# Later modulation weights with buffers and sums of their own, and stores and dependent loads issued from ScalarE's queue

## The chip, the cores and the metric

One core of a Trainium2 chip runs one program. The metric is the device time of a run in microseconds (us); of several runs the median is taken. The engines are TensorE (PE, matmuls; its weight loads are PEld), VectorE (DVE), ScalarE (ACT), GpSimd (POOL) and SyncE (SP), which here only issues DMAs. Each engine works its own list of instructions in order; semaphores hold an instruction until what it needs is there. TensorE's clock stands at one of two levels, 1.2 and 2.4 GHz; the profile gives the granted clock of a stretch as a share of the higher one.

## What is computed

One transformer block on 1024 tokens of 1024 channels, in float32. `dwconv` is a causal convolution along the tokens with one filter per channel, `wkv7_scan` a recurrence over the tokens with one 64x64 state per head (8 heads):

```python
mod = silu(c) @ ada_w + ada_b                 # 6 vectors of 1024
sh_m, sc_m, gt_m, sh_f, sc_f, gt_f = split(mod, 6)
h = rms_norm(x, mix_pre_g) * (1 + sc_m) + sh_m
p = h @ w_in                                  # u, u_gate | r, k, v, wd, ad, gd
u = silu(layer_norm(dwconv(u * sigmoid(u_gate), 31 taps)) * g + b)
r, k, v, ... = shift_mix(p)                   # p + (previous token's p - p) * mu
decay, a, kk = f(w0 + tanh(wd) @ w2), sigmoid(a0 + ad @ a2), unit(k * k_k)
y = layer_norm(wkv7_scan(r, decay, k, v, kk, a)) ; y = (y + bonus) * (sigmoid(gd) @ g2)
x = x + gt_m * rms_norm(concat(u, y) @ w_out, mix_post_g)
h = rms_norm(x, ffn_pre_g) * (1 + sc_f) + sh_f
z = dwconv(h @ w_up, 3 taps)                  # 2 x 2816 channels
x = x + gt_f * rms_norm((silu(z_gate) * z_val) @ w_down, ffn_post_g)
```

## The kernel before

**Layout.** Channels lie on the 128 partitions, tokens along the free axis, in two halves of 512 tokens. A tile of a projection is 128 output channels by 512 tokens in one PSUM bank. Float32 is reached by splitting each operand in a high and a low part: per 128 input channels three matmuls (lines 158 to 160), 24 for a tile of w_in. `weight` (line 134) fetches half a tile's weights, 128x512 or 256 KB: a DMA on SP (line 138), a cast to the high part on ScalarE (140), the low part on GpSimd (142). It draws on a pool of three buffers for each of the tags w, wh and wl, so at most three halves are under way.

**Modulation.** `mod` has twelve column blocks of 512, two (z = 0, 1) for each of the six vectors. Each is the sum of eight products: load a 128x512 slab of ada_w (line 226), multiply it by a column of silu(c) and add it to a running sum (lines 235 and 237, VectorE), then sum over the partitions with four matmuls against ones (`adr...`, line 243) and add the bias (244). The blocks of sh_m and sc_m come first, in `start`. The other eight blocks, 64 loads and products, are a generator, `spare`: `project` takes `rate` steps of it with each half of a tile (line 153). Groups 0 to 2 (gt_m, sh_f, sc_f; 48 loads) begin with the gated tiles of half 0, at three steps a half, later one; group 3 (gt_f, 16 loads) begins with the up-projection of half 0. Their slabs use the pool of three of the projection weights (tag w), their sum lies in SBUF (`cacc_b`), and their column sums take one of the two PSUM banks of tag m.

**Stages and order.** Half 0: `start`, six tiles begun early (`p_first`), `lora` (la), `in_group` for two groups of heads (k, v, r; `p_k`, `p_v`, `p_r`), gates (gd, ge), then four pairs of gated convolution tiles (`glu`: p_ug, p_u), whose result u goes to DRAM (line 320) and comes back with its edge as `cu` (line 333). Then the same for half 1, with the 31 taps of half 0's convolution as filler (`conv`: three channel tiles on VectorE with the sum in PSUM, line 344, one on ScalarE and GpSimd).

The recurrence runs in four units of 256 tokens, at the scheduler's highest priority. `unit` does, for two groups of heads, `prep` (decay w and a, line 492; scaled r, k, kk; score blocks s, line 550, stored to DRAM, 556), `inverse` (a triangular inverse done on blocks that are loaded in another layout, ab, line 575, and stored, sd, line 617), `finish` of the unit before (norm, bonus and gate: loads at 723 and 727, stores to `mixed` at 730) and `merge` (loads dd of the inverse, line 625, matmuls pt, 630, and hn, 637). `chain` then takes four steps (ch, lines 679 and 684; y, 692 to 702), each needing the state of the one before. Then out_proj of half 0 (stores md, 779), `channel_in` (residual, norm; stores x1d, 795), `up` of half 0: 44 tiles with 3-tap convolutions on VectorE and GpSimd, whose 22 products are stored (act, line 842), interleaved with the convolution of half 1; out_proj and channel_in of half 1, `down` of half 0, `up` and `down` of half 1.

**What sets the order.** A scheduler places each engine's instructions in one fixed list; `first()` and `high_priority` raise a stretch. A PSUM bank or an SBUF buffer is handed to its users in the order in which the program is written. PSUM has eight banks: tag m two, w two, and s, c, y and v one each. All DMAs shown here are issued by SP before the change.

Of the kernel before, what the change touches and what calls it, by code (L numbers as in the profile page):

```python
# [67 lines left out]
def build(nc, tc, I, O):  # L68
# [151 lines left out]
    def ada_cols(j, src, name, pool, tag, bufs, apool, atag, b="m", share=()):  # L220
# [23 lines left out]
        V.tensor_tensor(mod[:, j:j + 4], ps[:, 0:4], col("ada_b", j, 4), ALU.add)  # L244

    h = [None] * NK
    started = {}
# [65 lines left out]
    def glu(h, half, ct):  # L313
        pg = in_tile(h, 2 * ct + 1, f"ug{half}_{ct}")
        sg = tmp(f"sg{half}_{ct}")
        S.activation(sg, pg, AF.Tanh, scale=0.5, bias=ZERO)
        pu = in_tile(h, 2 * ct, f"u{half}_{ct}")
        u = tmp(f"u{half}_{ct}")
        V.scalar_tensor_tensor(u, sg, 1.0, pu, ALU.add, ALU.mult)
        nc.sync.dma_start(ud[half][ct], u)  # L320
        next(filler[0], None)
# [47 lines left out]
    def conv_norm(accs, half, b):  # L369
# [14 lines left out]
        for ct in range(4):  # L384
            V.tensor_tensor(accs[ct], accs[ct], rb, ALU.mult)
            t = slot(cv, "ctmp", f"th{half}_{ct}", bufs=2)
            S.activation(t, accs[ct], AF.Tanh, scale=col("ln_g", ct), bias=col("ln_b", ct))
            S.activation(accs[ct], accs[ct], AF.Identity, scale=col("ln_g", ct), bias=col("ln_b", ct))
            V.scalar_tensor_tensor(accs[ct], t, 1.0, accs[ct], ALU.add, ALU.mult)
            nc.sync.dma_start(mixed[half][ct], accs[ct])  # L390

# [35 lines left out]
    def gate_out(parts, half):  # L427
# [7 lines left out]
        for p in range(4):  # L435
            gb = bank(f"gt{half}{p}", "m")
            o = slice(p * P, (p + 1) * P)
            TE.matmul(gb, wh[:, o], gh, start=True, stop=False)
            TE.matmul(gb, wh[:, o], gl, start=False, stop=False)
            TE.matmul(gb, wl[:, o], gh, start=False, stop=False)  # L440
            TE.matmul(gb, w3[:, o], e3, start=False, stop=True)
            t = tmp(f"gt{half}_{p}")
            S.copy(t, gb)
            nc.sync.dma_start(gated[half][p], t)

# [31 lines left out]
    def prep(q, g, kvr, la, pcs, sa):  # L477
# [63 lines left out]
        s.bv = dr.tile([P, HT], F32, name=f"bvd{n}", tag="bvd", bufs=4)  # L541
        nc.sync.dma_start(s.bv, bv)

# [11 lines left out]
        for r, hh in HS:  # L555
            nc.sync.dma_start(sa[2 * g + hh].rearrange("c s t -> s c t"), at[r])

# [11 lines left out]
    def inverse(q, sa, sdg):  # L569
# [4 lines left out]
        for b in range(4):  # L574
            nc.sync.dma_start(ab3[b * 32:b * 32 + 32], sa5[b, b])
        dp = wk.tile([P, 528], F32, name=f"dm{q}", tag="dm", bufs=1)
# [37 lines left out]
        for x in range(2):  # L614
            sx = sdg[x].rearrange("q c (b r) (e t) -> b e (q c) r t", b=4, e=4)
            for b in range(4):
                nc.sync.dma_start(sx[b, b], dm[x][b * 32:b * 32 + 32])

    def merge(gs, sdg):

        for s in gs:
            s.dd = dd = wk.tile([P, 2, 8, 64], F32, name=f"dd{s.n}", tag="bk", bufs=2)
            for x in range(2):
                for r, hh in HS:
                    nc.sync.dma_start(dd[r, x], sdg[x, 2 * s.g + hh].rearrange("c r t -> r c t"))  # L625
        for s in gs:
# [81 lines left out]
    def finish(q, gs, ys):  # L708
# [11 lines left out]
        for s, y in zip(gs, ys):  # L720
            n = s.n
            bv = slot(rw, "t", f"bvl{n}", bufs=2)
            nc.sync.dma_start(bv, s.bv)
            gt = slot(rw, "t", f"gtl{n}", bufs=2)
            for i in range(2):
                p, o = 2 * s.g + i, slice(i * QT, (i + 1) * QT)
                nc.sync.dma_start(gt[:, o], gated[half][p][:, t0:t0 + QT])
                V.scalar_tensor_tensor(y[:, o], y[:, o], col("lnx_g", p), bv[:, o], ALU.mult, ALU.add)
                V.scalar_tensor_tensor(y[:, o], y[:, o], col("lnx_b", p), gt[:, o], ALU.add, ALU.mult)
                nc.sync.dma_start(mixed[half][4 + p][:, t0:t0 + QT], y[:, o])  # L730

# [39 lines left out]
    def out_proj(half, ins):  # L771

        acc = None
        for m in range(8):
# [3 lines left out]
            S.copy(t, ps)  # L778
            nc.sync.dma_start(md[half][m], t)
            acc = square_sum(acc, t, m, f"o{half}")  # L780
        return acc

    def channel_in(half, acc, b):
# [4 lines left out]
        for k in range(8):  # L788
# [5 lines left out]
            (V, G)[half == 0 and k % 2].tensor_tensor(t, t, xs[k], ALU.add)  # L794
            nc.sync.dma_start(x1d[half][k], t)
            acc = square_sum(acc, t, k, f"f{half}")
# [33 lines left out]
    def up(h, half, at=lambda j: None):  # L830

        acts = []
        for j in range(NU):
# [7 lines left out]
            if half == 0:  # L841
                nc.sync.dma_start(ad[j], g_)
            else:
# [45 lines left out]
    vt = v_tiles(0)  # L889
    kvrs = [in_group(h, 0, g, vt[g]) for g in range(2)]  # L890
    zero = tmp("zero", HT)
# [7 lines left out]
    with first():  # L899
        u0 = unit(0, kvrs, la)  # L900
        ys, zv = chain(0, *u0, None)
    ada = lambda gs: (x for g in gs for z in range(2)
                      for x in ada_cols(16 + 8 * g + 4 * z, I["ada2"][g, z], f"b{g}{z}", wp, "w", 3, cv, "cacc2"))
    spare, rate = ada(range(3)), 3
    for ct in range(4):
# [8 lines left out]
    for x in xs:  # L914
        V.tensor_tensor(x, x, rb, ALU.mult)
    h = [modulate(x, gm[:, k:k + 1], mod[:, k:k + 1], f"1_{k}") for k, x in enumerate(xs)]
    accs = [None] * 4
    rate = 1
# [18 lines left out]
    with first():  # L937
# [3 lines left out]
        finish(3, u3[0], ys)  # L941
    for _ in spare:
        pass
    gains()
# [4 lines left out]
    accs = [None] * 4  # L949
    spare = ada((3,))  # L950
    filler[0] = conv(1, accs, 3)
    up(h, 0, lambda j: j == 18 and conv_norm(accs, 1, "s"))
    V.tensor_tensor(gpf, mod[:, 40:48], col("ffn_post_g", 0, 8), ALU.mult)
# [70 lines left out]
```

## Time and profile before

| | |
|---|---|
| median of three runs | 1517.69 us (1516.13 to 1522.84) |
| profiled execution | 1514.99 us |
| its span | 1513.2 us |
| TensorE busy | 1377.6 us (91%), mean granted clock 0.949 |
| VectorE busy | 958.3 us (63%) |
| ScalarE busy | 645.9 us (43%) |
| GpSimd busy | 796.4 us (53%) |

The span is the time from the first to the last instruction in the profile. Busy shares are means over stages that have different limits; DMA issues and waits do not count as busy. The matmul of 512 columns is listed with some 0.39 us but the next starts 0.23 us after it, since they are pipelined.

### The profile page before, as it was taken

How to read it: one execution, taken by the hardware profiler on the slowest of the kernel's cores; microseconds unless marked ns; L12 is line 12 of the kernel's file. 1: busy time of each engine (PE TensorE's matmuls, PEld its weight loads, DVE VectorE, ACT ScalarE, POOL GpSimd, SP SyncE). 2: the span in 40 equal slices, each digit the busy share in tenths (PEclk: the TensorE clock that was granted, in tenths of full speed). 3: DMA queues.
4: the chain of work that ended last, by engine and by line, in shares of the span. 5: the costliest groups of instructions: out<-in, count | busy, mean ns of one | idle time of the engine just before them, and what ended most of it. 6: DMA issues, size and time to landing. Idle time of an engine off the chain costs nothing.

```text
span 1513.2 us, 22723 instructions
## 1 busy us (share of the span) xinstructions
PE 1377.6 (91%) x8148; PEld 1111.8 (73%) x8148; DVE 958.3 (63%) x1449; ACT 645.9 (43%) x1126; POOL 796.4 (53%) x710
## 2 busy tenths in 40 slices
PE   3999868789889999769999999999998999999995
PEld 2777657677667777657788887788886888888884
DVE  8657857969989576587889965557117555552102
ACT  5344322355534454344455555654233444443221
POOL 2555413676755346435577764446545555554443
PEclk9998998899999999869999999999999999999997
DMA  9153645533224544834444335884335333333332
GB/s 358 58 167 101 176 140 160 175 81 105 63 60 118 162 138 107 219 116 128 138 132 133 118 120 179 303 274 134 101 97 185 98 97 97 97 95 93 94 95 73
DMA packets 161761, 203.78 MB, mean 135 GB/s; under 512 B 63536, under 2 KB 70320, under 8 KB 161648
## 3 DMA queue, kind: packets, MB, share of 16 engines
q1 hardware_dynamic: 161648, 202.33, 43.4%
q8 instruction: 64, 1.05, 0.3%
q14 instruction: 49, 0.40, 0.1%
HBM read 168.19 MB, written 34.08 MB: 134 GB/s over the span
## 4 chain that ended last, share of the span: by engine, by line
PE 66%; DVE 17%; DMA 10%; issue 3%; SPq 2%; POOL 2%; ACT 1%; DVEq 0%; POOLq 0%; ACTq 0%
PE up L158 10%; PE up L159 9%; PE up L160 9%; PE d L159 5%; PE d L160 5%; PE d L158 5%; DMA w_adb<-ada 3%; DVE cv L344 2%; PE o L159 2%; PE o L158 2%; PE o L160 2%; DMA aw_ada<-ada 2%; DVE cacc_b L237 1%; DVE rkp L528 1%; SPq L625 1%
## 5 line engine op out<-in xcount | busy, mean ns | idle before, releaser
L142 POOL TENSOR_TENSOR wl_up<-w_up,wh_up 128x512 fp32r<-128x512 f32 x176 | 240.3, 1370 | 157.5 <-ACT wh_up L140 150.7
L158 PE MATMUL up<-hh_f,wh_up 128*128 128x512 f32 x704 | 278.6, 396 | 10.2 <-DVE q_za L815 7.0
L159 PE MATMUL up<-hl_f,wh_up 128*128 128x512 f32 x704 | 277.0, 394 | 0.0
L160 PE MATMUL up<-hh_f,wl_up 128*128 128x512 f32 x704 | 276.6, 393 | 0.0
L140 ACT CAST wh_up<-w_up 128x512 fp32r<-128x512 f32 x176 | 108.7, 619 | 187.0 <-PE up L159 127.6
L142 POOL TENSOR_TENSOR wl_dn<-w_dn,wh_dn 128x512 fp32r<-128x512 f32 x96 | 116.9, 1220 | 118.0 <-ACT wh_dn L140 112.0
L158 PEld LDWEIGHTS up<-hh_f,wh_up 128*128 128x128 f32 x704 | 133.9, 190 | 40.6 <-issue 9.8
L160 PEld LDWEIGHTS up<-hh_f,wl_up 128*128 128x128 f32 x704 | 133.6, 190 | 28.2 <-issue 0.2
L159 PEld LDWEIGHTS up<-hl_f,wh_up 128*128 128x128 f32 x704 | 133.7, 190 | 27.6
L159 PE MATMUL d<-al,wh_dn 128*128 128x512 f32 x352 | 139.4, 396 | 0.0
L160 PE MATMUL d<-ah,wl_dn 128*128 128x512 f32 x352 | 139.4, 396 | 0.0
L158 PE MATMUL d<-ah,wh_dn 128*128 128x512 f32 x352 | 139.2, 395 | 0.0
L344 DVE SCALAR_TENSOR_TENSOR cv<-cu,pv,cv 128x512 f32<-128x512 f32 x174 | 130.4, 749 | 2.4
L140 ACT CAST wh_dn<-w_dn 128x512 fp32r<-128x512 f32 x96 | 56.1, 584 | 151.3 <-PE d L159 123.7
L860 DVE TENSOR_SCALAR mo_f<-d,mod 128x512 f32<-128x512 f32 x16 | 12.0, 749 | 170.4 <-ACT q_sqd L859 159.1
L810 DVE SCALAR_TENSOR_TENSOR q_za<-up,pv,q_za 128x510 f32<-128x510 f32 x88 | 65.6, 746 | 78.4 <-ACT q_za L808 78.4
L352 POOL TENSOR_TENSOR cacc<-cacc,ctmp 128x512 f32<-128x512 f32 x60 | 79.1, 1318 | 42.3 <-ACT ctmp L351 38.7
L159 PEld LDWEIGHTS d<-al,wh_dn 128*128 128x128 f32 x352 | 66.2, 188 | 16.0
L160 PEld LDWEIGHTS d<-ah,wl_dn 128*128 128x128 f32 x352 | 66.2, 188 | 15.8
L158 PEld LDWEIGHTS d<-ah,wh_dn 128*128 128x128 f32 x352 | 66.2, 188 | 15.8
L838 DVE SCALAR_TENSOR_TENSOR q_za<-q_th,q_za 128x512 f32<-128x512 f32 x44 | 57.7, 1312 | 30.3 <-ACT q_th L837 30.3
L815 DVE SCALAR_TENSOR_TENSOR q_za<-up,pv,q_za 128x511 f32<-128x511 f32 x88 | 65.9, 748 | 14.0 <-ACT carry_z L814 8.3
(383 smaller groups left out, 3024.5 us busy)
## 6 DMA issues: line engine op xcount, KB each, us to landing
w_up<-w_up SPq DMA_DIRECT2D x176, 256.0 KB, 2.8
w_dn<-w_down SPq DMA_DIRECT2D x80, 256.0 KB, 2.7
w_adb<-ada SPq DMA_DIRECT2D x64, 256.0 KB, 3.0
aw_ada<-ada SPq DMA_DIRECT2D x32, 256.0 KB, 5.4
w_o<-w_out SPq DMA_DIRECT2D x32, 256.0 KB, 3.5
act<-q_za SPq DMA_DIRECT2D x22, 256.0 KB, 2.0
ax<-act SPq DMA_DIRECT2D x22, 256.0 KB, 4.2
w_ug<-w_in SPq DMA_DIRECT2D x16, 256.0 KB, 3.1
```

Of the source, the lines that this page charges most:

```text
L140: S.copy(hi, w)
L142: e.tensor_tensor(lo, w, hi.bitcast(F32), ALU.subtract)
L158: TE.matmul(ps, wh[:, o], xh, start=k == 0, stop=False)
L159: TE.matmul(ps, wh[:, o], xl, start=False, stop=False)
L160: TE.matmul(ps, wl[:, o], xh, start=False, stop=k == K - 1)
L237: V.scalar_tensor_tensor(acc, w, sc[:, k:k + 1], acc, ALU.mult, ALU.add)
L344: yield V.scalar_tensor_tensor(o, u[:, k:k + HT], cw(ct, k), acc, ALU.mult, ALU.add)
L352: G.tensor_tensor(acc, acc, t, ALU.add)
L528: V.tensor_tensor(pic(rkp[x][:, :, 1 + hh, :])[r], part(kkn, x)[r], half(eprev, x)[r], ALU.mult)
L810: V.scalar_tensor_tensor(a[:, 2:], ps[:, 0:HT - 2], fw(0), a[:, 2:], ALU.mult, ALU.add)
L815: V.scalar_tensor_tensor(a[:, 1:], ps[:, 0:HT - 1], fw(1), a[:, 1:], ALU.mult, ALU.add)
L838: V.scalar_tensor_tensor(g_, t, 1.0, g_, ALU.add, ALU.mult)
```

## The change

Two things are done at once. First, the later modulation weights get a generator of their own, `ada_rest`. Groups 0 to 2 load into five buffers of the convolution's pool that are free until `conv` starts, four loads ahead; group 3 into three buffers of tag k, two ahead. The running sum lies in PSUM (bank v, for group 3 bank c), the last product writes it to SBUF for the column sums, which now use the default bank tag, s, of one buffer. The generator is begun before the second `in_group` of half 0 with one step for each half of a tile, two in `glu`, and is emptied before half 0's convolution; group 3 begins at tile pair 8 of the up-projection. Second, at fifteen places `nc.sync.dma_start` becomes `S.dma_start`: the stores of u (line 320), of the mixed convolution (390), gated (444), bvd (542), sa (556), sd (617), mx (730), md (779), x1d (795) and act (842), and the loads ab (575), dd (625), bvl (723) and gtl (727), all of which wait for something computed. In SP's list 156 rows go and in ScalarE's 156 come. Lines of the changed kernel behind 245 have numbers higher by 31, from 888 on by some 40.

```diff
+    def ada_rest(groups, slab, ahead, last, b):
+
+
+        todo = [(g, z, k) for g in groups for z in range(2) for k in range(NK)]
+        tiles = {}
+
+        def fetch(i):
+            if i < len(todo):
+                g, z, k = todo[i]
+                tiles[i] = slab(i, f"adb{g}{z}_{k}")
+                nc.sync.dma_start(tiles[i], I["ada2"][g, z, k])
+
+        for i in range(ahead):
+            fetch(i)
+        for i, (g, z, k) in enumerate(todo):
+            fetch(i + ahead)
+            w, name = tiles.pop(i), f"b{g}{z}"
+            if k == 0:
+                acc = bank(f"ad{name}", b)
+                V.tensor_scalar(acc, w, sc[:, 0:1], None, ALU.mult)
+            else:
+                o = last(name) if k == NK - 1 else acc
+                V.scalar_tensor_tensor(o, w, sc[:, k:k + 1], acc, ALU.mult, ALU.add)
+            if k == NK - 1:
+                j = 16 + 8 * g + 4 * z
+                ps = bank(f"adr{name}")
+                for m in range(4):
+                    TE.matmul(ps[:, m:m + 1], o[:, m * P:(m + 1) * P], ones, start=True, stop=True)
+                V.tensor_tensor(mod[:, j:j + 4], ps[:, 0:4], col("ada_b", j, 4), ALU.add)
+            yield
...
             for b in range(4):
-                nc.sync.dma_start(sx[b, b], dm[x][b * 32:b * 32 + 32])
+                S.dma_start(sx[b, b], dm[x][b * 32:b * 32 + 32])
...
                 for r, hh in HS:
-                    nc.sync.dma_start(dd[r, x], sdg[x, 2 * s.g + hh].rearrange("c r t -> r c t"))
+                    S.dma_start(dd[r, x], sdg[x, 2 * s.g + hh].rearrange("c r t -> r c t"))
...
             if half == 0:
-                nc.sync.dma_start(ad[j], g_)
+                S.dma_start(ad[j], g_)
...
-    kvrs = [in_group(h, 0, g, vt[g]) for g in range(2)]
+    kvrs = [in_group(h, 0, 0, vt[0])]
+
+    ctags = ("ctmp", "cu", "ctmp", "cu3", "cacc0")
+    spare = ada_rest(range(3), lambda i, n: slot(cv, ctags[i % 5], n, 30 + HT if ctags[i % 5][:2] == "cu" else HT,
+                                                 2 if ctags[i % 5] == "ctmp" else 1)[:, :HT],
+                     4, lambda n: slot(cv, "cacc2", n), "v")
+    kvrs.append(in_group(h, 0, 1, vt[1]))
...
-    ada = lambda gs: (x for g in gs for z in range(2)
-                      for x in ada_cols(16 + 8 * g + 4 * z, I["ada2"][g, z], f"b{g}{z}", wp, "w", 3, cv, "cacc2"))
-    spare, rate = ada(range(3)), 3
+    rate = 2
...
+    for _ in spare:
+        pass
...
-    for _ in spare:
-        pass
...
-    spare = ada((3,))
     filler[0] = conv(1, accs, 3)
-    up(h, 0, lambda j: j == 18 and conv_norm(accs, 1, "s"))
+
+    def between(j):
+        nonlocal spare
+        if j == 8:
+            spare = ada_rest((3,), lambda i, n: slot(rw, "k", n, bufs=3), 2, lambda n: slot(cv, "cacc2", n), "c")
+        if j == 18:
+            conv_norm(accs, 1, "s")
+
+    up(h, 0, between)
```

TensorE's list where unit 0's decay projection stands (w, tile numbers from the program; p_first, p_k and p_v are projection tiles), before:

```order
L159 MATMUL p_first_303<-hl_7_454,wh_r_4_639 128x512
L160 MATMUL p_first_303<-hh_7_451,wl_r_4_641 128x512
L492 MATMUL w_1170<-la_556,w2a_79 128x256 x2
L160 MATMUL p_first_322<-hh_4_436,wl_k_4_665 128x512
L158 MATMUL p_first_322<-hh_5_441,wh_k_4_663 128x512
L159 MATMUL p_first_322<-hl_5_444,wh_k_4_663 128x512
L160 MATMUL p_first_322<-hh_5_441,wl_k_4_665 128x512
```

and with the change:

```order
L158 MATMUL p_k_912<-hh_5_441,wh_k_4_936 128x512
L159 MATMUL p_k_912<-hl_5_444,wh_k_4_936 128x512
L160 MATMUL p_k_912<-hh_5_441,wl_k_4_938 128x512
L158 MATMUL p_k_912<-hh_6_446,wh_k_4_936 128x512
L159 MATMUL p_k_912<-hl_6_449,wh_k_4_936 128x512
L523 MATMUL w_1242<-la_556,w2a_79 128x256 x2
L160 MATMUL p_k_912<-hh_6_446,wl_k_4_938 128x512
L158 MATMUL p_k_912<-hh_7_451,wh_k_4_936 128x512
```

The first w has moved from the last tiles of p_first to the fifth projection tile behind them (p_r, p_k, p_v, p_r stand whole between, and four rows adrb with the column sums of two modulation blocks).

TensorE's list at unit 1's merge (pt and hn), before:

```order
L158 MATMUL p_k_3527<-hh_5_3252,wh_k_4_3548 128x512
L159 MATMUL p_k_3527<-hl_5_3255,wh_k_4_3548 128x512
L630 MATMUL pt_2785<-dd_2775,at_2505 64x64
L160 MATMUL p_k_3527<-hh_5_3252,wl_k_4_3550 128x512
L158 MATMUL p_k_3527<-hh_6_3257,wh_k_4_3548 128x512
L630 MATMUL pt_2785<-dd_2775,at_2505 64x64 x15
L630 MATMUL pt_2803<-dd_2780,at_2631 64x64 x16
L159 MATMUL p_k_3527<-hl_6_3260,wh_k_4_3548 128x512
L160 MATMUL p_k_3527<-hh_6_3257,wl_k_4_3550 128x512
L158 MATMUL p_k_3527<-hh_7_3262,wh_k_4_3548 128x512
L159 MATMUL p_k_3527<-hl_7_3265,wh_k_4_3548 128x512
L160 MATMUL p_k_3527<-hh_7_3262,wl_k_4_3550 128x512
```

and with the change:

```order
L159 MATMUL p_r_3831<-hl_7_3277,wh_r_4_3852 128x512
L160 MATMUL p_r_3831<-hh_7_3274,wl_r_4_3854 128x512
L169 MATMUL c_y_2736<-cst,t_ysq_2732 128x2 x4
L169 MATMUL c_y_2736<-cst,t_ysq_2733 128x2 x4
L661 MATMUL pt_2797<-dd_2787,at_2517 64x64 x16
L661 MATMUL pt_2815<-dd_2792,at_2643 64x64 x16
L187 MATMUL rb_y_2750<-cst,t_yx_2749 128x128 x4
L668 MATMUL hn_0_2833<-dd_2787 64x64 x16
L668 MATMUL hn_0_2851<-dd_2792 64x64 x2
L187 MATMUL rb_y_2758<-cst,t_yx_2757 128x128 x4
L668 MATMUL hn_0_2851<-dd_2792 64x64 x14
L668 MATMUL hn_1_2869<-at_2517,dd_2787 64x64 x6
```

Before, the merge's matmuls stand among those of a projection tile; now the last projection tile ends ahead of them, and none follows until the recurrence's first step is issued.

ScalarE's list at unit 0's merge (dd<-pt is the merge's copy, wh_... are casts of projection weights), before:

```order
L140 CAST wh_ug_1_4_2084<-w_ug_1_4_2082 128x512
L316 ACTIVATE q_sg_1_2116<-p_ug_1_2054,small 128x512
L631 COPY dd_1462<-pt_1472 128x512
L510 ACTIVATE t_ksq_2579<-cacc_k_753,small,pv 128x256 x2
L631 COPY dd_1467<-pt_1490 128x512
L140 CAST wh_u_1_0_2121<-w_u_1_0_2119 128x512
L140 CAST wh_u_1_4_2148<-w_u_1_4_2146 128x512
```

and with the change, at the same merge:

```order
L140 CAST wh_u_3_0_2391<-w_u_3_0_2389 128x512
L351 DMA u_2_486<-q_u_2_2333 128x512
L648 DMA sd_482<-dm_1499 32x16x16 x8
L656 DMA dd_1534<-sd_482 64x8x64 x4
L656 DMA dd_1539<-sd_482 64x8x64 x4
L662 COPY dd_1534<-pt_1544 128x512
L525 ACTIVATE einv_cs_2442<-w_2440,pv 128x256 x2
L347 ACTIVATE q_sg_3_2386<-p_ug_3_2336,small 128x512
L140 CAST wh_u_3_4_2411<-w_u_3_4_2409 128x512
```

The stores of u and sd and the loads dd have come in ahead of the copy, and the cast of wh_u_3_4 stands behind all of them.

## Rows read from the trace of the kernel before

**Rows 1.** The page's part 4, shares of the chain by engine.

```profile
PE 66%; DVE 17%; DMA 10%; issue 3%; SPq 2%; POOL 2%; ACT 1%; DVEq 0%; POOLq 0%; ACTq 0%
```

**Rows 2.** Busy time by stage (columns as in the first row).

```profile
core 0: us, PE busy (x) PEld busy (x) DVE busy (x) ACT busy (x) POOL busy (x), PEclk, DMA share, GB/s
120.00:340.00 220.00, 181.70 (x1355) 143.73 (x1354) 161.33 (x278) 78.94 (x142) 105.30 (x102) 0.88 0.49 140
340.00:620.00 280.00, 263.72 (x2241) 206.60 (x2238) 220.74 (x388) 132.80 (x244) 158.18 (x136) 0.96 0.38 109
620.00:740.00 120.00, 94.86 (x903) 78.62 (x903) 91.63 (x133) 50.17 (x94) 57.35 (x44) 0.82 0.50 153
740.00:940.00 200.00, 199.06 (x879) 163.89 (x878) 161.26 (x206) 105.94 (x194) 133.44 (x98) 0.99 0.42 134
```

**Rows 3.** The same view in slices of 20 us.

```profile
80.00:100.00 20.00, 20.00 (x98) 16.81 (x97) 9.52 (x15) 8.10 (x13) 13.10 (x14) 1.00 0.62 207
120.00:140.00 20.00, 17.26 (x72) 14.39 (x71) 11.66 (x20) 9.20 (x17) 13.98 (x17) 0.76 0.32 94
200.00:220.00 20.00, 10.21 (x139) 8.00 (x136) 13.96 (x19) 2.87 (x6) 3.81 (x3) 0.83 0.46 144
340.00:360.00 20.00, 18.60 (x218) 15.13 (x214) 19.75 (x36) 10.15 (x17) 12.90 (x14) 0.91 0.46 151
380.00:400.00 20.00, 15.57 (x77) 10.64 (x76) 19.66 (x26) 7.87 (x13) 16.39 (x12) 0.83 0.21 67
```

**Rows 4.** The chain of waits, 192 to 276 us: shares, then start, length, what.

```profile
by line: DMA w_adb<-ada 36.0%; DVE cacc_b L237 14.0%; issue 6.2%; DVE bk L530 5.0%; DVE rkp L528 3.6%; DMA w_u<-w_in 3.5%; DVE bk L533 3.3%; PE adrb L243 3.2%; SPq L625 3.0%; DVE a L531 2.0%; DVE cacc_b L235 1.8%; DVE einv_cs L498 1.8%; SPq
...
205.39 3.32 DMA w_adb<-ada
208.80 1.82 DVE cacc_b L237
210.64 2.83 DMA w_adb<-ada
...
222.16 0.68 PE ch L679 x14
```

**Rows 5.** Timeline of TensorE: start, length, instruction; last, line 684 alone.

```profile
70.64 1.13 PE L492 MATMUL w<-la,w2a 64*128 64x256 f32 x4
...
76.82 0.39 PE L158 MATMUL p_r<-hh,wh_r 128*128 128x512 f32 x1
77.05 0.39 PE L159 MATMUL p_r<-hl,wh_r 128*128 128x512 f32 x1
...
296.52 0.79 PE L158 MATMUL p_la<-hh,wh_la 128*128 128x512 f32 x1
...
372.00 0.45 PE L679 MATMUL ch<-zv,rkp 128*64 128x64 f32 x8
...
L684 PE MATMUL ch<-rs,at x16: 218/218/267, 380.9 to 381.4; 64*64 64x64 f32 x16
```

**Rows 6.** Waits of SP's queue: line, releaser, us in total, times, longest.

```profile
SPq L842 <- DVE q_za L840: 49.5, 22, 4.4
...
SPq L556 <- DVE at L552: 31.8, 14, 8.5
...
SPq L226 <- DVE cacc_b L237: 28.6, 28, 3.5
...
SPq L730 <- DVE ys L729: 15.2, 10, 3.2
...
SPq L617 <- DVE dm L612: 11.5, 3, 6.7
```

**Rows 7.** Timeline of SP, 182 to 195 us.

```profile
182.63 5.64 SPq L617 DMA_DIRECT2D sd<-dm  x8
...
189.05 5.41 SPq L625 DMA_DIRECT2D dd<-sd  x8
```

**Rows 8.** Answers by line: L237 (whole, 200 to 300 us), L344, L625's landing, L842.

```profile
L237 DVE SCALAR_TENSOR_TENSOR cacc_b<-w_adb,sc,cacc_b x56: 720/752/1873, 145.0 to 728.9; 128x512 f32<-128x512 f32 x56
...
  DMA w_adb<-ada: 15.9, 16
...
L344 DVE SCALAR_TENSOR_TENSOR cv<-cu,pv,cv x174: 726/748/758, 321.6 to 873.9; 128x512 f32<-128x512 f32 x174
...
DMA to landing us min/median/max: 2.6/3.2/5.4
...
L842 SPq DMA_DIRECT2D act<-q_za x22: 320/326/327, 697.7 to 951.6; - x22
```

**Rows 9.** The chain of waits, 612 to 695 us.

```profile
617.74 0.60 SPq L625
...
625.21 5.53 DMA q_xr<-xT
...
683.60 2.71 DMA w_adb<-ada
...
687.11 2.87 DMA w_adb<-ada
```

**Rows 10.** Waits of ScalarE, longest first.

```profile
ACT wh_up L140 <- PE up L159: 127.6, 93, 3.8
```

More of the change, by code (lines that the diff above doesn't have):

```diff
@@ L319, in glu @@
         V.scalar_tensor_tensor(u, sg, 1.0, pu, ALU.add, ALU.mult)
-        nc.sync.dma_start(ud[half][ct], u)
+        S.dma_start(ud[half][ct], u)
         next(filler[0], None)
@@ L389, in conv_norm @@
             V.scalar_tensor_tensor(accs[ct], t, 1.0, accs[ct], ALU.add, ALU.mult)
-            nc.sync.dma_start(mixed[half][ct], accs[ct])
+            S.dma_start(mixed[half][ct], accs[ct])
     def lora(h, half):
@@ L443, in gate_out @@
             S.copy(t, gb)
-            nc.sync.dma_start(gated[half][p], t)
+            S.dma_start(gated[half][p], t)
     v3 = lambda t: t.rearrange("p (c t) -> p c t", c=8)
@@ L541, in prep @@
         s.bv = dr.tile([P, HT], F32, name=f"bvd{n}", tag="bvd", bufs=4)
-        nc.sync.dma_start(s.bv, bv)
+        S.dma_start(s.bv, bv)
         s.at = at = wk.tile([P, 8, 64], F32, name=f"at{n}", tag="at", bufs=4)
@@ L555, in prep @@
         for r, hh in HS:
-            nc.sync.dma_start(sa[2 * g + hh].rearrange("c s t -> s c t"), at[r])
+            S.dma_start(sa[2 * g + hh].rearrange("c s t -> s c t"), at[r])
         bf = bk.rearrange("p c x t -> p c (x t)")
@@ L574, in inverse @@
         for b in range(4):
-            nc.sync.dma_start(ab3[b * 32:b * 32 + 32], sa5[b, b])
+            S.dma_start(ab3[b * 32:b * 32 + 32], sa5[b, b])
         dp = wk.tile([P, 528], F32, name=f"dm{q}", tag="dm", bufs=1)
@@ L722, in finish @@
             bv = slot(rw, "t", f"bvl{n}", bufs=2)
-            nc.sync.dma_start(bv, s.bv)
+            S.dma_start(bv, s.bv)
             gt = slot(rw, "t", f"gtl{n}", bufs=2)
@@ L726, in finish @@
                 p, o = 2 * s.g + i, slice(i * QT, (i + 1) * QT)
-                nc.sync.dma_start(gt[:, o], gated[half][p][:, t0:t0 + QT])
+                S.dma_start(gt[:, o], gated[half][p][:, t0:t0 + QT])
                 V.scalar_tensor_tensor(y[:, o], y[:, o], col("lnx_g", p), bv[:, o], ALU.mult, ALU.add)
                 V.scalar_tensor_tensor(y[:, o], y[:, o], col("lnx_b", p), gt[:, o], ALU.add, ALU.mult)
-                nc.sync.dma_start(mixed[half][4 + p][:, t0:t0 + QT], y[:, o])
+                S.dma_start(mixed[half][4 + p][:, t0:t0 + QT], y[:, o])
     x1d = [[dr.tile([P, HT], F32, name=f"x1{half}_{k}") for k in range(8)] for half in range(2)]
@@ L778, in out_proj @@
             S.copy(t, ps)
-            nc.sync.dma_start(md[half][m], t)
+            S.dma_start(md[half][m], t)
             acc = square_sum(acc, t, m, f"o{half}")
@@ L794, in channel_in @@
             (V, G)[half == 0 and k % 2].tensor_tensor(t, t, xs[k], ALU.add)
-            nc.sync.dma_start(x1d[half][k], t)
+            S.dma_start(x1d[half][k], t)
             acc = square_sum(acc, t, k, f"f{half}")
```

## Prediction

> **What bounds the kernel now.** I read the page's chain shares first, then busy time by stage, then the chain inside the stage that idles, then SP's waits. The chain is TensorE for 66% of the span, VectorE for 17% and DMA for 10% [rows 1]. The stages [rows 2] say where the other third sits: from 740 us on TensorE is busy 199.06 of 200 us at a granted clock of 0.99, so nothing is to be had there, whereas in 120 to 340 it is busy 181.70 of 220 at 0.88, in 340 to 620 263.72 of 280 at 0.96, in 620 to 740 94.86 of 120 at 0.82. The idle time is 38.3 + 16.3 + 25.1 = 79.7 us, and the low clock costs about 0.12 x 220 = 26 us more of the first stage alone. That is the pool from which any gain comes.
>
> In the first stage the worst slice is 200 to 220 with 10.21 us of TensorE [rows 3]. The chain of 192 to 276 us is, to 36.0%, the wait for a modulation weight (w_adb) and to 14.0% the product that consumes it [rows 4]: load 3.32, product 1.82, load 2.83, and so on, one at a time. The reason is the shared weight pool of three: SP holds the next load until a product has freed a slot, 28.6 us in 28 waits [rows 6], and the projection weights queue behind it. VectorE itself waits 15.9 us for these loads between 200 and 283 [rows 8]. After 340 the first limit is another: VectorE is busy 19.75 and 19.66 of 20 us in two of the slices [rows 3].
>
> **Part one: own buffers for the later weights.** All 48 loads and products of groups 0 to 2 stay; they move from 140 to 284 us to the stretch behind 60 us. VectorE is busy 9.52 and 11.66 of 20 us in two slices there [rows 3], room for 48 x 0.752 = 36 us of products [rows 8] spread over some 110 us. With the sum in PSUM a product reads one operand there; no row shows this product so, and the nearest is the convolution tap, which sums in PSUM too and takes 0.749 us [rows 8] against 0.752: I take no difference, with 0.1 us either way (48 x 0.1 = 5 us, on an engine with room) as bounds.
>
> But the column sums now draw on the one bank "s", which the units' decay projection (w, L492) uses too, and that bank is handed out in program order. The order shows the result: unit 0's first w stood before the last tiles of p_first, at 70.64 us, and now stands after two sums of eight products each, 20 matmuls into the fifth tile from 76.82 us on [rows 5]. A tile of 24 matmuls at the 0.23 us between the two starts there is 5.45 us, so w starts at 76.8 + 4.8 x 5.45 = 103 us: 32 us later. Unit 0's inversion and merge slide behind the projections.
>
> How far that goes, in steps. Up to unit 0's merge the order has 16.5 tiles from 76.8 us on, 90 us, and I put the small matmuls between them at 30 us (the same ones fill the difference between tiles and busy time of before), which ends at 196. The merge then wants its sd stores and dd loads: 5.64 + 5.41 us of issue [rows 7] and about 5 us of landing, now behind casts on ScalarE; I put its start at 218 and, since before needed 33 us from the dd issue at 189.05 [rows 7] to the first chain step at 222.16 [rows 4], unit 0's first chain step at 245: 23 us late. Against that, the projections are ahead: la, which began at 296.52 [rows 5], is nearly done by 250. Next, before took 380.9 - 222.2 = 159 us from that chain step to unit 1's (372.00, its second half at 380.9 [rows 5]), with sixteen tiles and 28 products in it. After has eight tiles (44 us), no products, and conv taps instead; the limit is VectorE at 85 to 92 us, then a merge of unit 1 into which no projection tile falls any more, because the half-tile k of unit 2 has no free slot: some 45 us. 245 + 90 + 45 = 380: level with before. By then about 16 conv taps more are done (12 us of VectorE) and about a tile (5 us of TensorE). Since VectorE limits what follows, I count **10 us gained** (bounds 45 gained, if the merge is not held up, and 15 lost, if the lag of 23 us stays and only 8 are made up).
>
> The 16 loads of group 3 leave the up-projection's start: there the chain goes load 2.71, load 2.87 between 683 and 690 [rows 9], while the weights of up wait. I take **5 us gained** (2 to 8). They return at j >= 8, where TensorE is full and VectorE is busy 161.26 of 200 us [rows 2]: 16 x 0.752 = 12 us of products come into some 45 us that have 9 us free, so **2 us lost** (0 to 6).
>
> **Part two: 156 DMA issues from ScalarE.** SP loses what waits for VectorE: the act stores 49.5 us, the at stores (L556) 31.8, the finish stores (L730) 15.2, the sd stores (L617) 11.5 [rows 6]; a weight load can no longer stand behind eight dd loads of 5.41 us [rows 7]. At 617 us that gain is on the path: dd issues, then the residual's load that ends in 5.53 us [rows 9]; **3 us gained** (0 to 6). The price is on ScalarE, whose order is fixed: whatever it waits for now holds the casts behind it. In unit 0 the store u, eight sd and eight dd issues and the copy from pt stand ahead of the cast wh_u_3_4; in unit 1 no cast stands between rows 250 and 292 of its order. ScalarE's casts wait for TensorE 127.6 us in up [rows 10], so there the 22 act stores of 0.326 us each [rows 8] are covered and I cost them at nothing (uncovered: 22 x 0.326 = 7 us). Before 680 the cover is two halves of a tile: a stall beyond about 5 us reaches TensorE. Of the 31.8 + 15.2 + 11.5 us that SP waited, I let one in ten pass for the queue's own waits in units 0 to 3: **6 us lost** (0 to 18).
>
> The Trainium skill bears on this part. In "DMA: Bandwidth & Descriptors", section "Issuing engines are not separate DMA queues", it says that starting DMAs from several engines saves only the sequencer's issue time, usually small beside the transfer. The trace agrees only in part: 5.41 us of issue for eight dd loads is longer than the 3.2 us in which one lands [rows 8]. In "PSUM — Partial Sum Buffer", section "Engine vs sequencer instructions", ScalarE's queue is called strictly first in, first out: by it every wait in the moved rows would stand in front of casts, and part two would lose the upper end, 18 us, instead of 6.
>
> **Sum.** 10 + 5 - 2 + 3 - 6 = 10 us gained. The profiled execution took 1514.99 us, so 1505 for it; the median of the runs, 1517.69, is 2.7 above, and the forecast for the median is 1507.7.
>
> **Rivals.** *The merge isn't held up.* If the recurrence of unit 0 starts no later than the order forces (103 us is early enough, since TensorE had its worst slices only from 200 us on) and the freed slots keep the projections fed, the 38 us of idle time in the first stage go, and with part of the low clock the gain is 45: 1472. For it speaks that the chain of 192 to 276 is half load and product [rows 4]; against it, that VectorE is nearly full right behind. Chance 0.17. *The lead is given back.* ScalarE's waits take 14 to 18 instead of 6: within 3 us of 1516. For it: the four units each have some ten rows waiting for VectorE in ScalarE's queue. Chance 0.2. *Slower.* Bank "s" decides: the first chain step of unit 0 comes 23 us late or more, the four units' recurrences follow one another, and TensorE stands through unit 1's merge of 45 us with nothing to fill it, so that 25 are lost and 8 made up; with 6 lost on ScalarE and the gain of 6 in channel_in and up: 1517.7 + 25 - 8 + 6 - 6 = 1535. It decides from the point where unit 1's second half step lies after about 395 us. For it speaks that before filled this very merge with projections [rows 5]; against it, that the filled work is not lost but done earlier. Chance 0.2. *It doesn't do what it says*: the loads still come one by one, since four ahead at 3 us a landing is less than a weight tile's pace needs. Then only part two is left, -3 + 6: 1521. The order has the loads far ahead, so 0.03.
>
> **How the numbers follow.** The forecast of 1507.7 has 0.40. A measurement of this kernel can tell about 0.5%, 7.6 us. Below 1510.1: the first rival and about four fifths of the forecast's own spread, 0.17 + 0.33 = 0.50. Within 7.6: the rest of the forecast, the last rival and most of the lead given back, 0.07 + 0.03 + 0.17 = 0.27. Above 1525.3: the slower rival and the end of the lead given back, 0.20 + 0.03 = 0.23. The forecast's own range is 1497 to 1517; for 8 in 10 it reaches far towards the first and the slower rival, 1476 to 1533.
>
> **What would show it.** Right: no wait of SP or VectorE for w_adb between 140 and 300; la of half 1 begins near 240 instead of 296.52; unit 0's first chain step near 245, unit 1's second half step within 10 us of 381 with a TensorE gap of about 40 us before it; VectorE over 19 of 20 us behind it; up starting some 10 us sooner, its first weights not behind w_adb. Wrong: unit 1's step before 350 (the first rival) or after 395 (the third); waits on ScalarE for VectorE at L587, L648 and L761 of the changed kernel that together pass 15 us and end in TensorE waiting for a cast; or a loss in up at j >= 8 of more than 6 us.

## The result

The changed kernel is slower: 1558.55 us median of four runs (1552.39 to 1560.92) beside 1518.14, a ratio of 1.0268 with a 95% interval of 1.0228 to 1.0308, so some 40 us lost where 10 us of gain were forecast. (The places of part two are fourteen, not fifteen as the section on the change says.) The profiled execution's span is 1550.6 us, 37.4 more than before. The page of the changed kernel, its shares of the chain by engine, by the line beside [rows 1]:

```profile
PE 57%; DVE 26%; DMA 8%; issue 3%; ACT 2%; ACTq 2%; POOL 1%; DVEq 0%; SPq 0%; POOLq 0%
```

VectorE has gone from 17% to 26% of the chain. Busy time of the changed kernel between six points that both kernels pass (unit 0's first chain step, unit 1's merge, the second half of unit 1's first step, out_proj of half 0, its last norm, up, the end), columns as in [rows 2]:

```profile
254.00:374.00 120.00, 94.15 (x718) 73.20 (x715) 100.39 (x170) 53.55 (x93) 78.01 (x75) 0.86 0.23 61
374.00:413.00 39.00, 28.16 (x384) 22.79 (x386) 20.52 (x45) 14.16 (x27) 13.63 (x11) 0.72 0.22 62
413.00:565.00 152.00, 139.76 (x1160) 110.52 (x1157) 101.56 (x185) 63.72 (x119) 68.08 (x59) 0.92 0.36 103
565.00:665.00 100.00, 89.62 (x720) 69.48 (x720) 60.47 (x117) 38.59 (x74) 44.58 (x36) 0.93 0.46 133
665.00:700.00 35.00, 21.35 (x290) 19.29 (x290) 21.79 (x37) 9.11 (x18) 7.72 (x6) 0.66 0.53 174
700.00:1550.00 850.00, 810.30 (x3762) 659.87 (x3762) 462.39 (x593) 368.20 (x635) 470.86 (x396) 0.98 0.40 129
```

and of the kernel before between the same points:

```profile
221.00:338.00 117.00, 99.67 (x741) 80.38 (x737) 87.60 (x147) 44.78 (x81) 63.88 (x62) 0.87 0.45 130
338.00:381.00 43.00, 41.60 (x468) 33.92 (x469) 40.15 (x68) 24.69 (x44) 28.47 (x29) 0.96 0.34 106
381.00:543.00 162.00, 148.46 (x1206) 115.14 (x1205) 132.50 (x225) 71.22 (x129) 88.88 (x75) 0.95 0.37 105
543.00:627.00 84.00, 79.82 (x677) 62.39 (x675) 52.16 (x103) 39.02 (x75) 43.34 (x33) 1.00 0.52 133
627.00:665.00 38.00, 25.22 (x347) 22.75 (x347) 29.41 (x45) 11.94 (x23) 10.28 (x8) 0.61 0.70 238
665.00:1513.00 848.00, 811.36 (x3746) 662.47 (x3746) 461.56 (x586) 367.76 (x633) 468.06 (x396) 0.97 0.41 129
```

The stretches last 120 us instead of 117, 39 instead of 43, 152 instead of 162, 100 instead of 84, 35 instead of 38, 850 instead of 848. With the 33 us by which the first of them starts late (254 instead of 221) that is the whole loss: **33 late at the start, 10 regained behind unit 1, 13 lost again in out_proj and the norm.** What the forecast was to show is there: TensorE's timeline has la of half 1 at 241.75 instead of 296.52 [rows 5], and unit 0's decay projection w (line 523 now, 492 before) where the order had put it; line 715 is the second half of a chain step:

```profile
105.45 0.91 PE L523 MATMUL w<-la,w2a 64*128 64x256 f32 x3
...
241.75 0.49 PE L158 MATMUL p_la<-hh,wh_la 128*128 128x512 f32 x1
...
L715 PE MATMUL ch<-rs,at x16: 311/311/366, 412.6 to 413.4; 64*64 64x64 f32 x16
```

105.45 stands against 70.64 and 412.6 against 380.9 [rows 5].

### The profile page after: what moved, and what is told of

It is laid out like the page before. It is cut to its first block, busy times and chain, and to the rows that moved or that the text cites. A ratio compares the mean times of both kernels' runs of the same rounds, so it can differ in the third digit from the quotient of the medians.

```text
span 1550.6 us, 22698 instructions
## 1 busy us (share of the span) xinstructions
PE 1384.2 (89%) x8148; PEld 1117.8 (72%) x8148; DVE 938.4 (61%) x1449; ACT 645.1 (42%) x1126; POOL 791.4 (51%) x710
## 4 chain that ended last, share of the span: by engine, by line
PE 57%; DVE 26%; DMA 8%; issue 3%; ACT 2%; ACTq 2%; POOL 1%; DVEq 0%; SPq 0%; POOLq 0%
PE up L158 6%; PE up L159 6%; PE up L160 6%; DVE cv L375 6%; PE d L160 5%; PE d L158 5%; PE d L159 5%; DMA aw_ada<-ada 2%; DVE q_za L846 2%; PE o L159 1%; DVE q_za L841 1%; PE o L158 1%; PE o L160 1%; DVE rkp L559 1%; DVE q_za L869 1%
```

## Experiments

Two suspects came out of this: bank s, which makes the recurrence late (theory A), and ScalarE's queue, which holds what stands behind waiting DMA rows (theory B). All ratios below are to the kernel before on the same chip. In the diffs of whole groups one line stands for all.

**Each part alone.** Part one: every `S.dma_start` of the change goes back.

```diff
-                S.dma_start(ad[j], g_)
+                nc.sync.dma_start(ad[j], g_)
```

> Part one alone: the later modulation weights with own buffers and sums, all stores and dependent loads on SyncE's queue as before. Theory A (the one bank s, handed out in program order, sends unit 0's decay projection behind two modulation sums, and everything in the recurrence comes some 33 us late): unit 0's first chain step near 250 us, unit 1's second half step near 408 instead of 380.9, time 1545 to 1560. Theory B (waits in ScalarE's queue hold the casts, part two is the loss): the step near 222 to 230, time 1503 to 1518.

Measured: 1529.53 us, ratio 1.0103 (1.0079 to 1.0127). Part two: the kernel before with the fourteen places on ScalarE.

> Part two alone: the kernel before with the fourteen places issued from ScalarE's queue, modulation weights in the shared pool as before. Theory A: unit 0's first chain step near 222 us, time within 8 us of before, 1510 to 1526. Theory B: the time of the changed kernel, 1545 to 1560, with TensorE waiting for casts behind waiting DMA rows.

Measured: 1538.86 us, 1.0152 (1.0128 to 1.0175). Both parts lose, and neither theory alone gave both times: A expected a larger loss from part one and nothing from part two, B the reverse.

**Each suspect undone in the changed kernel.** First the bank:

```diff
-                ps = bank(f"adr{name}")
+                ps = bank(f"adr{name}", "m")
```

> The changed kernel with one edit: the column sums of ada_rest take a bank of tag m (two buffers, as before the change) instead of the one of tag s. Theory A: unit 0's decay projection back at some 71 us, its first chain step within 8 us of 222, the loss gone, 1500 to 1522. Theory B: 1545 to 1560 unchanged, since ScalarE's queue is as in the changed kernel.

Measured: 1520.59 us, 1.0040 (1.0025 to 1.0055). Then the block traffic (at, sd, ab, dd) back on SyncE's queue:

```diff
-                S.dma_start(sx[b, b], dm[x][b * 32:b * 32 + 32])
+                nc.sync.dma_start(sx[b, b], dm[x][b * 32:b * 32 + 32])
```

> The changed kernel with the unit's block traffic (stores at and sd, loads ab and dd) back on SyncE's queue; the rest of part two stays on ScalarE. Theory A: the first chain step stays near 250 us and the time at 1545 to 1560. Theory B: ScalarE no longer waits for the sd stores and dd loads, time 1510 to 1530.

Measured: 1522.73 us, 1.0050 (1.0029 to 1.0071). A's time was right on the first, B's on the second: there are two losses. The next four tell whether they are separate; their edits are those of above put together, in p1_bank_m part one alone with tag m, in both_m_recur_sp also

```diff
-            S.dma_start(bv, s.bv)
+            nc.sync.dma_start(bv, s.bv)
```

and so for bvd, gtl and mx.

> Part one alone with the column sums in tag m: nothing issued from ScalarE. Theory C (two separate losses: bank s delays the recurrence, the block traffic holds up ScalarE; each is undone by its own edit): the 14 us of part one alone go and its gain shows, 1500 to 1512, unit 0's first chain step within 8 us of 222. Theory D (the early products themselves delay the units on VectorE, the bank is only one way in which they do): 1518 to 1530.

Measured: **1490.73 us, 0.9871 (0.9849 to 0.9894)**. Part one alone with the other bank beats both kernels, by more than theory C's 1500 to 1512 allowed; theory D falls.

> Both parts with both suspects undone: column sums in tag m, at, sd, ab and dd on SyncE's queue. Theory C: the losses add, so 1520.6 - 8 (what the other stores on ScalarE gave beside part one alone) and less, 1490 to 1512, faster than before. Theory D: no better than either undone alone, 1518 to 1524.

Measured: 1508.40 us, 0.9983 (0.9965 to 1.0001): in theory C's range, but level with before and not faster.

> As the kernel with both suspects undone, and finish's traffic (bvd, bvl, gtl, mx) on SyncE's queue as well; ScalarE keeps u, the mixed convolution, gated, md, x1d and act. If what waits for VectorE on ScalarE's queue is the cost (C), out_proj and channel_in of half 0 lose their wait for mx and gtl rows ahead of the casts: 3 to 10 us below both_m_units_sp. If only the block traffic costs: the same within 3 us.

Measured: 1496.60 us, 0.9914 (0.9894 to 0.9935): 11.8 us below both_m_units_sp, a little more than the 3 to 10.

> The kernel before with part two without the unit's block traffic: ten of the fourteen places on ScalarE, weights as before. Theory C: the 24 us of part two alone came from the block traffic, so 1505 to 1518. Otherwise, if any store on ScalarE's queue costs: 1525 to 1540.

Measured: 1522.43 us, 1.0088 (1.0055 to 1.0120), above the 1518 that theory C allowed: something in the other ten places costs too.

The size of each loss can now be read in pairs. **Bank s**: 1.0103 against 0.9871 without part two, 1.0268 against 1.0040 with it, 2.3% both times (1.0050 against 0.9983, 0.7%, with the block traffic on SyncE). **Part two**: 1.0152 on the kernel before, 1.0268 / 1.0103 = 1.0163 on part one, 1.0040 / 0.9871 = 1.0171 with bank m: 1.5 to 1.7% in three kernels with different lists. Its ten places other than the block traffic have no such steady price: 1.0088 on the kernel before, 1.0050 / 1.0103 = 0.9948 on part one, a gain, and 0.9983 / 0.9871 = 1.0113 with bank m. Start times of the same points in the profiled executions, in us, from TensorE's timeline:

| kernel | unit 0: w | unit 0: step | unit 1: 2nd half step | out_proj | up | span |
|---|---|---|---|---|---|---|
| before | 70.6 | 221.3 | 380.9 | 543.5 | 664.8 | 1513.2 |
| changed | 105.5 | 254.3 | 412.6 | 565.2 | 700.6 | 1550.6 |
| p1_only | 104.0 | 244.8 | 398.6 | 548.1 | 676.6 | 1525.6 |
| p2_only | 71.8 | 221.5 | 407.9 | 562.0 | 698.9 | 1541.8 |
| both_bank_m | 70.7 | 227.1 | 382.7 | 534.4 | 668.1 | 1519.2 |
| both_units_on_sp | 104.0 | 248.2 | 396.9 | 542.0 | 667.6 | 1515.2 |
| p1_bank_m | 70.3 | 216.6 | 361.8 | 515.1 | 637.3 | 1487.1 |
| m_sd_dd_act | 71.0 | 217.6 | 354.6 | 529.6 | 655.4 | 1500.5 |
| m_late_start | 71.9 | 215.9 | 372.8 | 524.7 | 660.5 | 1512.2 |

Every kernel in which the column sums of `ada_rest` take bank s has w at 104 to 105.5 and its first step 23 to 33 us late; in the rows with bank m (the last three and both_bank_m) w is at 70 to 72 and the step within 6 us of before. Against its pair with bank m such a kernel is still late at the start of up: p1_only by 39 us against p1_bank_m, the changed kernel by 33 against both_bank_m, and, with the block traffic on SyncE, both_units_on_sp by 8 against both_m_units_sp (659.7).

**Which rows of part two cost.** From here on the base is p1_bank_m, and one group of rows goes to ScalarE at a time. First the sd stores and dd loads, the act stores, and two edits to part one itself: its start, where the lines that make `spare` move behind unit 0's code and `rate = 2` there becomes `rate = 3`, and the start of group 3:

```diff
-        if j == 8:
+        if j == 0:
```

> Part one with column sums in tag m, and of part two the sd stores and dd loads of inverse and merge alone, eight and eight issues in each of four units. Theory C: ScalarE is held for some 10 to 13 us in each unit by waits and issue, and of this 2 to 5 us reach TensorE: 1499 to 1511. If issue time alone counts: the same as p1_bank_m, since SyncE's 11 us of issue a unit are saved as well.

Measured: 1510.01 us, 0.9985 (0.9964 to 1.0006): 1.1% above p1_bank_m, as theory C expected.

> Part one with column sums in tag m, and of part two the 22 act stores of the up-projection alone. If any store on ScalarE costs (waits for VectorE ahead of casts): 0.2 to 0.6% above p1_bank_m, 1494 to 1500 beside its 1490.7. If only rows ahead of casts in the units cost, as the prediction costed it (cover of 127.6 us): level with p1_bank_m within 0.2%.

Measured: 1490.67 us, 0.9866 (0.9834 to 0.9899): level.

> Part one with column sums in tag m, but begun where the kernel before begins it, with the gated tiles of half 0 at three steps a half: own buffers and PSUM sums without the earlier start. If the gain of part one comes from the buffers: 1490 to 1497. If it comes from using VectorE's idle time between 60 and 140 us: 1503 to 1512.

Measured: 1512.44 us, 0.9999 (0.9979 to 1.0018). The time is just above the range expected if the early start were the gain, but the edit didn't take the early start away: SyncE issues the first load at 34.6 us (34.7 in p1_bank_m, 135.5 in the kernel before), and in both kernels 15 of the 48 products run before 100 us. Only then do they part, with 16 products before 160 us instead of 26. So how much of part one's gain is due to the buffers and how much to the early start stays open. Up to unit 1's merge the kernel is level with p1_bank_m (TensorE's first pt at 321.3 and 322.5; 338.0 before). It loses 23 us between there and up, a stretch in which neither kernel has a modulation product; the scheduler's list is another there, and it isn't settled what in it costs.

> Part one with column sums in tag m and group 3 begun with the up-projection instead of at its ninth pair. The prediction took 5 us gained at the start of up and 2 lost behind it for the later start: by that 3 us more than p1_bank_m, 1492 to 1497. If up is bound by TensorE in both places: level.

Measured: 1503.04 us, 0.9942 (0.9922 to 0.9962): 0.7% slower than p1_bank_m, which neither expectation had, while up begins at 637.3 and 637.4. In this kernel the slice of 20 us behind 680 us and the chain of waits in it read

```profile
680.00:700.00 20.00, 14.36 (x124) 12.77 (x125) 12.94 (x20) 3.58 (x8) 4.42 (x3) 0.51 0.51 165
...
687.54 0.77 DVE adb L268
688.33 2.67 DMA k_adb<-ada
691.10 0.77 DVE adb L268
691.88 2.95 DMA k_adb<-ada
694.93 0.76 DVE cacc_b L268
```

beside, in p1_bank_m,

```profile
680.00:700.00 20.00, 20.00 (x163) 15.55 (x162) 17.52 (x23) 11.22 (x22) 11.29 (x10) 1.00 0.39 130
```

Load, product, load stand in line again, although the loads are issued two ahead; TensorE is busy 14.36 instead of 20.00 us, and its granted clock is 0.51 of 2.4 GHz, the lower of the two levels, in a slice in which it idles 5.6 us.

Since every edit makes the scheduler write a new list, the next run measures what that alone does (the diff), and the others take the remaining rows, group by group, by `nc.sync.dma_start` becoming `S.dma_start`.

```diff
-                     4, lambda n: slot(cv, "cacc2", n), "v")
+                     3, lambda n: slot(cv, "cacc2", n), "v")
```

> Part one with column sums in tag m, loads three ahead instead of four. It changes no wait that the trace of p1_bank_m shows, but the scheduler writes another list, so it measures what another list alone is worth. If lists alone move the time by 1% the verdicts on single rows of part two mean little: below 1480 or above 1502. If by less than 0.3%, differences of 0.4% and more between edits are their own: 1487 to 1495.

Measured: 1494.67 us, 0.9884 (0.9850 to 0.9918), 0.13% from p1_bank_m; it is the only edit of this kind.

> Part one with column sums in tag m, and of part two finish's rows alone on ScalarE (loads bvl and gtl, stores mx; 32 rows, each store behind VectorE's ys). If waiting is the price: 0.4 to 0.9% above p1_bank_m, 1496 to 1504. If issue time is the price (32 x 0.4 us): level.

Measured: 1493.12 us, 0.9872 (0.9845 to 0.9899): level, against the waiting theory. The bvd stores stay on SyncE here.

> Part one with column sums in tag m, and of part two the stores md and x1d alone on ScalarE. md follows ScalarE's own copy, so it waits for nothing new: level with p1_bank_m within 0.3%, or a gain of up to 3 us in channel_in. If any store costs: 1495 to 1500.

Measured: 1492.41 us, 0.9869 (0.9837 to 0.9901): level.

> Part one with column sums in tag m, and of part two the stores u, mixed convolution and gated alone on ScalarE. gated follows ScalarE's own copy, u and mixed wait for VectorE, 8 rows each: within 0.3% of p1_bank_m by the waiting theory (u waits about 1 us a time); 1496 or more if any store costs.

Measured: 1499.51 us, 0.9927 (0.9887 to 0.9966): 0.6% above, with intervals that just overlap.

> Part one with column sums in tag m, and of part two the at stores and ab loads alone on ScalarE (16 and 16 rows). The stores wait for VectorE's at (31.8 us on SyncE before), the loads for the stores. If waits in ScalarE's queue cost as with sd and dd: 0.4 to 1.1% above p1_bank_m, 1496 to 1507. If only sd and dd cost, because the merge's copy and the projection's casts stand directly behind them: level within 0.2%.

Measured: 1497.04 us, 0.9907 (0.9890 to 0.9924): 0.4% above, again with intervals that just overlap.

> Part one with column sums in tag m, and of part two the eight u stores alone on ScalarE. If u is what costs 0.5% in m_u_mix_gate_act (it waits for VectorE's gated product ahead of the next tile's casts): 1496 to 1502. If not, gated or mixed is, or the list: level within 0.2%.

Measured: **1485.55 us, 0.9836 (0.9809 to 0.9864)**, the fastest of all and below both expectations; its interval overlaps that of p1_bank_m. So u alone isn't what costs in m_u_mix_gate_act; whether gated, mixed or the list does was not tried.

**How sd and dd cost.** ScalarE's timeline of the changed kernel at unit 3's merge (ACTq are its DMA issues, in brackets the idle time before an instruction and its releaser):

```profile
642.50 0.73 ACT L745 ACTIVATE t_ysq<-ys,small 128x512 f32<-128x512 f32 x1 [3.03 <-DVE dm L643]
644.86 4.42 ACTq L648 DMA_DIRECT2D sd<-dm  x8
649.33 0.72 ACT L745 ACTIVATE t_ysq<-ys,small 128x512 f32<-128x512 f32 x1 [6.10 <-DMA sd<-dm]
649.41 7.05 ACTq L656 DMA_DIRECT2D dd<-sd  x8
656.51 0.59 ACT L809 COPY q_m<-o 128x512 f32<-128x512 f32 x1 [6.45 <-DMA dd<-sd]
656.99 0.62 ACT L140 CAST wh_up<-w_up 128x512 fp32r<-128x512 f32 x1
```

From 643.2 to 656.5 ScalarE does one thing of 0.72 us. The eight sd issues wait for VectorE's dm, the eight dd issues for the stores to land, and out_proj's copy q_m and the casts of up stand behind them. TensorE pays in two places: c_y waits for t_ysq, which stands behind sd, and pt waits for dd. TensorE's waits (line, releaser, us in total, times, longest), of p1_bank_m and then of m_sd_dd_act, two kernels whose programs differ only in the queue of the sd stores and dd loads:

```profile
PE pt L661 <- DMA dd<-sd: 1.8, 2, 1.6
...
PE c_y L169 <- ACT t_ysq L745: 1.7, 1, 1.7
```

```profile
PE pt L661 <- DMA dd<-sd: 14.0, 11, 5.8
...
PE c_y L169 <- ACT t_ysq L745: 6.3, 2, 3.8
```

3.5 us have become 20.3, and the run is 1.1%, some 17 us, longer. For part two as a whole this path explains less. The two rows in the changed kernel and then in p1_only, where every one of these rows is on SyncE:

```profile
PE pt L661 <- DMA dd<-sd: 18.9, 10, 7.7
...
PE c_y L169 <- ACT t_ysq L745: 13.6, 3, 5.9
```

```profile
PE pt L661 <- DMA dd<-sd: 14.1, 11, 4.0
...
PE c_y L169 <- ACT t_ysq L745: 7.8, 2, 6.3
```

That is 32.5 us against 21.9, 10.6 of the 25 us that part two costs there. In p2_only, the kernel before with part two, pt waits 6.3 us for dd (6.2 before) and c_y has no row in either, so its loss of 1.5% came another way.

## Why the prediction was wrong

**Right: what the order did.** w was put at 103 us and came at 105.45, unit 0's merge at 218 and came at 222.8, la near 240 and came at 241.75. Unit 0's first step was put at 245 and came at 254.3; with part one alone it came at 244.8, so that the other 9 us came with part two. In that merge the dd issues took 8.74 us of ScalarE for the 5.41 of SyncE [rows 7]. (218 and the 33 us that the sum names would give 251; those 33 us run from the dd issue, which stood ahead of the merge.)

**Wrong: the step "the limit is VectorE at 85 to 92 us, ... 245 + 90 + 45 = 380: level with before".** It let the lag of 23 us be made up on the way from unit 0's first step to unit 1's second half step: 135 us for a way that had taken 159. That way took 158.3 us, and the lag stayed: 412.6 instead of 380.9. The merge at its end, put at 45 us, took 39; the part before it, put at 90, took 120. VectorE, the limit named, was busy 100.39 us of them and not 85 to 92, and some 20 us in which it idled were put at nothing. By 413 us 17 more convolution taps had run than before by 381, as put, but nearly all of them stood ahead of the merge: 54 taps with 40.44 us, where before had 15 with 10.60. Line 375 in the stretch of 120 us and line 344 in the 117 us of before (length, busy time and number of the taps, then clock, DMA share and GB/s), and the shares of the chain of waits in the stretch of the changed kernel:

```profile
254.00:374.00 120.00, 40.44 (x54) 0.86 0.23 61
221.00:338.00 117.00, 10.60 (x15) 0.87 0.45 130
```

```profile
by line: DVE cv L375 28.4%; DVE rkp L559 5.8%; DVE bk L561 4.8%; DVE t_dx L638 4.2%; ACTq L648 3.2%; issue 3.1%; ACTq L656 2.7%; DMA cu<-u 2.6%; DVE v L337 2.0%; DVE zv L725 2.0%; DVE at L583 2.0%; PE p_la L159 1.9%; DVE mq L584 1.9%; DVE r
```

The chain runs mostly over VectorE, where taps stand between the unit's own operations. Nor was so much work taken out of the way as the sum had it: by the matmuls of line 159, eight to a tile, it held 9.4 projection tiles against 12.6 before, not eight against sixteen, and before had 24 products in it, not 28.

That the lag isn't made up later either is shown by the edit of bank s. The changed kernel is behind both_bank_m by 27 us at unit 0's first step, 30 at unit 1's second half step, 31 at out_proj, 33 at up and 31 at the end, and p1_only behind p1_bank_m by 28, 37, 33, 39 and 38.5. It can be made up in another list: both_units_on_sp is behind both_m_units_sp by 29 us at the step, 19 at unit 1, 20 at out_proj, 8 at up and 7 at the end. What sets the length of the way isn't settled: from the step to unit 1's merge p1_only took 117 us and both_units_on_sp 108, with some 40 us of taps each, p1_bank_m 106 with 22 us, and m_sd_dd_act 87 with none. The 10 us that the forecast put down to the lead did come behind that point (152 us instead of 162), but p2_only, which has no lead from part one, took 154 there; that the number agrees isn't shown to be more than luck.

**Mis-sized: ScalarE's loss.** "6 us lost (0 to 18)" was 1.5 to 1.7%, 23 to 26 us, in three kernels. The working took a tenth of SyncE's old waits and looked for stalls of casts. TensorE's waits for a cast sum to 6.2 us at most in the kernels with part two or a part of it (p2_no_units), and the changed kernel shows none; for the sd and dd rows the cost came with the merge's own path, pt and c_y, which the working had not followed, although it named the copy in the same queue. The nearer sentence was the one from the Trainium skill, "PSUM — Partial Sum Buffer", section "Engine vs sequencer instructions": with ScalarE's queue strictly first in, first out, every wait stands in front of what follows, and 18 us would be lost. At unit 3's merge the trace agrees, with the 13.3 us of ScalarE above; but not every wait that stands there costs time, since finish's rows were level. The prediction also cited the Trainium skill, "DMA: Bandwidth & Descriptors", section "Issuing engines are not separate DMA queues", for the sentence that issuing from another engine only saves issue time, usually small beside the transfer. The runs agree as far as the gain goes: the 3 us credited to channel_in did not come, and out_proj to up took 135.5 us instead of 121.3 (125.8 with sd and dd alone on ScalarE, 122.2 with all on SyncE). The prediction found the trace to agree only in part, but it set eight issues, 5.41 us, beside the 3.2 us of one landing; one issue is 0.68 us.

**Up: the act stores right, group 3 not.** Act stores on ScalarE at nothing: level (0.9866 and 0.9871). Group 3's later start was put at 5 - 2 = 3 us gained, and none of it came: from up to the end the changed kernel took 850 us, p1_only 849 and p1_bank_m 850, beside 848 before. That m_group3_at_once is 0.7% slower says only that with tag k's buffers the start at once costs some 10 us.

**The rival.** The slower case named bank s, and that half is shown; its sign, unit 1's second half step after 395, came. Its price of 1535 took 25 us for the start and 8 made up, which came as 32 and 10, but let channel_in and up pay back what ScalarE costs. The two losses were held to be nearly alternatives (a chance of 0.2 each), and as whole parts they add: part one and part two alone give 1.0103 x 1.0152 = 1.0257, measured together 1.0268.

**Open.** How part two costs 1.5% on the kernel before, where the waits of pt and c_y hardly change; why its ten places other than the block traffic lose on two kernels and gain on a third; and which of them costs, since finish's rows, md with x1d, and act cost nothing by themselves, while bvd, gated and the mixed convolution were never moved alone (bvd and finish's rows together, taken back to SyncE in both_m_recur_sp, gave 0.7%). It is open too how much of each single row's figure is the scheduler's list, since m_late_start lost 23 us in a stretch without modulation products, while m_three_ahead moved 0.13%. The signs on bank s and on part two as a whole don't hang on that: they are the same in all three pairs of each.

## What to carry to other kernels

A buffer that is handed out in program order is an edge in the schedule: before giving a new, low-priority user the only bank of a tag, look at which urgent user stands behind it, and read the order for the first instruction of the longest dependent sequence. Cost such a sequence from its start to its end with the filler that the order puts between its steps, and let it make up time only where a row shows what would shorten it. Before moving DMA rows that wait to another engine's queue, look at what stands behind them there. A dependent store and load in the middle of that engine's work held it for both landings here and cost 1.1%, while act, md with x1d and finish's rows cost nothing that could be measured; that a row waits did not tell by itself which it would be.

## What the runs showed of the hardware

Eight dd issues took 5.41 us on SyncE [rows 7] and 5.47 to 8.74 us on ScalarE in the changed kernel, where no single issue took more than 0.66 us; what held the longer groups the profile doesn't show. Nothing else was unexpected in kind: in the changed kernel's 665 to 700 us, with TensorE busy 21.35 of 35 us, the granted clock was 0.66, and in 700 to 1550 us, with 810.30 of 850 us, it was 0.98.
